# A decoder layer with routed experts: two kinds of DRAM writes move to another queue, and the embedding's four pieces move along the program

## The chip, the cores and the metric

The kernel runs on 1 core of one Trainium2 chip. Its engines are TensorE (PE, with its weight loads shown as PEld), VectorE (DVE), ScalarE (ACT), GpSimd (POOL) and SyncE (SP); each works through its own queue in order, and a DMA (a transfer between DRAM and SBUF) is issued from the queue of SP, ACT or POOL. The metric is device time in microseconds (us), less is better. The kernel before takes 1480.44 us, the median of 3 runs (1479.26 to 1485.14).

## The reference, cut to what matters

One layer over 512 tokens of width 2048, all float32:

```
y = concat(s5(u), conformer_conv(v, g)) @ w_o + b_o
h = layer_norm(ALPHA * x + y)                        # residual 1
# routing: softmax over 4 groups, top 1; 8 experts in it, top 2
t = h;  g_p, g_idx = top_1(softmax(t @ w_rg + b_rg))
e_val, e_idx = top_2(t @ w_re + b_re, within the group)
combine = softmax(e_val) * g_p
m = sum_e combine[e] * ((silu(t @ w_gate[e]) * (t @ w_up[e])) @ w_down[e])
h = layer_norm(ALPHA * h + m)                        # residual 2
e = (p @ w_p) * sigmoid(h @ w_pg + b_pg)             # p: (512, 256), the embedding
x = layer_norm(ALPHA * h + e)
```

There are 32 experts of hidden width 256, and each expert's three matrices are 6 MB, so the expert stage reads 192 MB of weights.

## The kernel before, in words

The tokens are NT = 4 tiles `tt[m]` of 128 rows. The kernel runs in stages: input projection and the two head groups, output projection with the first norm, routing, the expert stage, and the tail with the gate product and the last norms. This change is in the routing and at the start of the expert stage.

At the end of the output projection `finish` and `normalize` turn `tt[m]` into h; line 877 writes each tile to DRAM (`h_dram`, 1 MB each) from ACT's queue, since the experts fetch their tokens from there by an indirect gather. The routing is a chain of small DVE and PE steps: choices (`oh`, line 955), counts (lines 958 to 966 on PE), the rank of each chosen expert (`rtok`, line 991), one-hot rows (`slot_hot`), and two small products (lines 196 and 203) that give the slot tables `sl0` (whom to gather) and `wt0` (their weights).

The embedding's product p @ w_p depends on nothing of this. Its four row pieces m = 0 to 3 are placed where PE may be idle: `embedding(m, x)` (line 828 on) builds a zero `z` from column `x`, adds it to piece m of p on ACT (line 833), so that the product can't start before `x` exists, multiplies (line 839), copies the result out of PSUM on ACT (line 840) and writes it to `p_dram` in two writes of 512 KB (line 841, ACT's queue). Before, piece 0 is tied to a column of the logits `lg`, piece 1 to `cmax` (line 1033), piece 2 to `wt0`. Piece 3 stands behind the first expert group, lines 1172 to 1179; there the copies go into a tile `pe` that exists once, so the second pair of copies waits until the first write has been read out.

The expert stage has 13 groups (`GROUPS`); group 0 has two experts that are fixed beforehand, the others are read from a table that the routing makes. A group gathers its token rows (line 1069, POOL's queue, into `gx`), transposes them (`xtp`, line 1083), runs up and gate (`gu`, line 1103), the activation, and down (`dps`, line 1123), and scatters 2 x 512 KB to `y_dram` (line 1073, POOL's queue). Weights come in loads of 1 MB from SP's queue (line 1065) into a ring of 17 tiles: 15 named `ring`, and the 2 `raw` tiles, which hold w_p until the embedding's last product and join the ring behind it. The loads of group 0 (12) and the first three of group 1 are issued first.

Behind group 0 stands a branch, `tc.If(most > 0)` at line 1187, for tokens that don't fit; here it isn't taken. Every engine goes through it, and SP's way through waits until the transfers that ACT and SP have issued have landed. The tile framework places the instructions of each engine in an order of its own, and gives the DMAs of ACT and SP together eight completion counters in turn, so that at most eight of them are in flight and each one waits for the one eight places ahead; POOL's DMAs have eight others.

Lines that matter: 828 to 841, 877, 912 (piece 0), 1037 and 1038 (pieces 1 and 2), 1069, 1073, 1128 (clearing `gx`), 1148 to 1155, 1172 to 1181, 1187.

Of the kernel before, what the change touches and what calls it, by code (L numbers as in the profile page):

```python
# [8 lines left out]
FT = mybir.dt.float32  # L9
# [8 lines left out]
P = 128  # L18
# [8 lines left out]
NT = S // P  # L27
NE = 32
FH = 256
ALPHA = 2.0 ** 0.25  # L30
# [24 lines left out]
def build(tc, I, out, dbg=None, stages=9):  # L55
    nc = tc.nc
    V = nc.vector
    A = nc.scalar
    G = nc.gpsimd
    T = nc.tensor  # L60
# [147 lines left out]
    h_dram = dpool.tile([S, D], FT, name="h_dram")  # L208
    p_dram = dpool.tile([NT, 4, P, 512], FT, name="p_dram")
# [6 lines left out]
    wt0 = cpool.tile([P, NGR], FT, name="wt0")  # L216
# [27 lines left out]
    def bank(name, bufs=1):  # L244
        if name in bturn:

            n = bturn[name]
            bturn[name] += 1
            name, bufs = (("zp", 4) if n % 5 < 4 else ("xp", 1)) if name == "ops" else (("wps", "cps")[n % 2], 1)
        return psA.tile([P, 512], FT, name=name, tag=name, bufs=bufs)  # L250

    if True:
        with ExitStack() as s2:
# [151 lines left out]
            for j in range(3):  # L405
                m = 1 << j
# [191 lines left out]
            for s_, f in enumerate(order):  # L598
# [17 lines left out]
                ps = w_in_mm(w_first if s_ == 0 else next(w_in))  # L616
# [19 lines left out]
    tt = [tp_.tile([P, D], FT, name=f"tt{m}") for m in range(NT)]  # L636
    s1 = top.enter_context(ExitStack())
    if True:
# [36 lines left out]
        ps = bank("htp")  # L675
# [30 lines left out]
        rs_, ps = rows  # L706
# [3 lines left out]
        for q in range(4):  # L710
            hl = next(w_in)
            for f in range(2):
                wh, wl = hl[f]
                ps = bank("ops")
# [22 lines left out]
        with ExitStack() as s3:  # L737
# [24 lines left out]
            ps = bank("yp")  # L762
# [22 lines left out]
        with ExitStack() as s3:  # L785
# [5 lines left out]
            lg = op_.tile([P, NT, 36], FT, name="lg")  # L791
# [36 lines left out]
            def embedding(m, x):  # L828

                z = op_.tile([P, 1], FT, name="pz0", bufs=1)  # L830
                V.tensor_scalar(z, x, 0.0, 0.0, op0=OP.is_equal, op1=OP.mult)
                pm = wB.tile([P, 2, P], FT, name="pm", tag="whi", bufs=4)
                A.activation(pm, pT[:, :, m * P:(m + 1) * P], AF.Identity, bias=z)
                for q in range(2):
                    pe_ = wB.tile([P, 2, 512], FT, name="pe", tag="wlo", bufs=4)
                    for c in range(2):
                        ps = bank("ops")
                        for k in range(2):
                            T.matmul(ps, pm[:, k], wps[q][:, k, c * 512:(c + 1) * 512], start=k == 0, stop=k == 1)
                        A.copy(pe_[:, c], ps)  # L840
                    A.dma_start(p_dram[m, 2 * q:2 * q + 2].rearrange("c p d -> p c d"), pe_)

            def logits(m, c):

# [27 lines left out]
            def normalize(m, mean, rstd):  # L872
                for q in range(4):
                    i = slice(q * 512, (q + 1) * 512)
                    t = tt[m][:, i]
                    layer_norm(t, t, mean, rstd, g1[:, i], b1[:, i])
                A.dma_start(h_dram[m * P:(m + 1) * P], tt[m])
                dump("h", tt[m], lambda d: d[m * P:(m + 1) * P])

            for c in range(4):  # L880
# [5 lines left out]
                ps = [bank("ops") for _ in range(NT)]  # L886
# [20 lines left out]
            pT = wB.tile([P, 2, S], FT, name="pT", tag="whi", bufs=4)  # L907
            nc.sync.dma_start(pT, I["pT"])
            wps = []
            for q in range(2):  # L910
                wps.append(raw_load(I["w_p"][q]).rearrange("p (k n) -> p k n", k=2))
            embedding(0, lg[:, NT - 1, 0:1])


            rp = Carve(scr)
# [67 lines left out]
            over, rtok, wts = sv[:, 0], sv[:, 1], sv[:, 2].rearrange("p (j t) -> p j t", j=2)  # L983
# [5 lines left out]
            V.tensor_reduce(pos, pt2, axis=AX.X, op=OP.add)  # L989
            V.tensor_tensor(pt, oo, rr[:, 0:NE].unsqueeze(1).unsqueeze(1).broadcast_to(e2), op=OP.mult)  # L990
            V.tensor_reduce(rtok, pt2, axis=AX.X, op=OP.add)
            by_place, pw = rp1.tile([P, 2 * NT, NP], FT), rp.tile([P, 2 * NT, NP], FT)
            pb = [P, 2 * NT, NP]
            V.tensor_tensor(by_place, rank.unsqueeze(1).broadcast_to(pb), rtok.unsqueeze(2).broadcast_to(pb), op=OP.is_equal)
# [34 lines left out]
            gcn, cmax = rt("gcn", NP), rt("cmax", 1)  # L1029
# [4 lines left out]
            V.tensor_copy(tab[:, NP:2 * NP], gcn)  # L1034
            V.tensor_copy(tab[:, 2 * NP:], cmax)
            A.dma_start(sv_dram, sv.rearrange("p a n -> p (a n)"))
            embedding(1, cmax)
            embedding(2, wt0[:, 0:1])
            dump("sl0", sl0); dump("wts", wts)

    psA_.close()
# [5 lines left out]
    if True:  # L1047
        psE = s5.enter_context(tc.tile_pool(reuse_waits="tile", name="psE", bufs=1, space=PSUM))
        ep = s5.enter_context(tc.tile_pool(reuse_waits="tile", name="ep", bufs=1))
# [95 lines left out]
            return [ring_load(part(expert(i, j), q)) for j in range(len(GROUPS[i][1]))]  # L1145

        early = [loads(0, q) for q in range(6)]
        pm3 = ep.tile([P, 2, P], FT, name="pm3")
        nc.sync.dma_start(pm3, I["pT"][:, :, (NT - 1) * P:])
        for m in range(NT):  # L1150
            A.mul(tt[m], tt[m], ALPHA)
        gather(sl0[:, 0:1])
        V.tensor_copy(ids_, tab[:, 0:NP])
        columns()
        for i, (width, members) in enumerate(GROUPS):
# [13 lines left out]

            ahead1 = [loads(1, q) for q in range(3)]  # L1170

            for q in range(2):
                pe_ = ep.tile([P, 2, 512], FT, name="pe")
                for c in range(2):
                    ps = bank("dps", 4)
                    for k in range(2):
                        T.matmul(ps, pm3[:, k], wps[q][:, k, c * 512:(c + 1) * 512], start=k == 0, stop=k == 1)
                    (A.copy if c else V.tensor_copy)(pe_[:, c], ps)
                A.dma_start(p_dram[NT - 1, 2 * q:2 * q + 2].rearrange("c p d -> p c d"), pe_)
            ring.extend(rpool.tile([P, D], FT, name="raw", tag="raw", bufs=2) for _ in range(2))  # L1180
            ahead1 += [loads(1, q) for q in range(3, 5)]

# [63 lines left out]
    with ExitStack() as s5:  # L1246
# [28 lines left out]
        for n in range(8):  # L1275
            ps = bank("fps", 6)
# [187 lines left out]
```

## Time and profile before

| | |
|---|---|
| median of 3 runs | 1480.44 us |
| profiled execution: its time, its span | 1482.75 us, 1480.9 us |
| PE busy | 1262.3 us (85%) |
| DVE, ACT, POOL busy | 778.5, 372.5, 382.7 us |
| moved | 349.34 MB, 236 GB/s over the span |
| mean granted TensorE clock | 0.926 |

In 40 slices of 37 us of the span, the DMA engines and what they moved look so:

```
DMA  6344445445632351147799999999999986426413
GB/s 233 112 131 118 150 122 156 142 117 174 246 123 85 114 210 57 44 170 284 298 422 420 420 420 416 418 417 414 415 411 411 411 351 235 142 107 213 142 44 121
```

From slice 20 on, at about 740 us, they move 411 to 422 GB/s for twelve slices: this is the expert stage. The rows further down are of the stretch just ahead of it, 600 to 745 us, and of the stage itself. Times in them are us from the start of the span. A row of the timeline is: start, duration, engine, line and operation, what it writes and reads, how many in a row, and in brackets how long the engine stood idle before it and what ended that.

### The profile page before, as it was taken

What the parts mean: (1) busy time and instruction counts of PE and PEld (TensorE: products, weight loads), DVE (VectorE), ACT (ScalarE), POOL (GpSimd) and SP (SyncE); (2) the same over time, 40 slices, a digit from 0 to 9 for tenths busy, and PEclk for the clock granted to TensorE, in tenths of its full rate; (3) what the DMA queues carried; (4) which work ended last, traced back from release to release, by engine and by line L of the source; (5) the groups of instructions that cost most, each with busy time, mean ns of one, the idle gap of its engine ahead of it and who ended that gap; (6) DMA issues with size and microseconds to landing.
All of it is one profiled execution on the core that took longest, in us unless ns stands there. A gap on an engine that the chain in (4) does not pass through costs nothing. (4 is left out here: it accounts for less than half of the span.)

```text
span 1480.9 us, 16676 instructions
## 1 busy us (share of the span) xinstructions
PE 1262.3 (85%) x6206; PEld 805.9 (54%) x6207; DVE 778.5 (53%) x1251; ACT 372.5 (25%) x559; POOL 382.7 (26%) x313
## 2 busy tenths in 40 slices
PE   6999999998999999968598998777676775599996
PEld 4887877887777888844243332221111111388884
DVE  7999899879998653681111110000000006985467
ACT  4335565544433432031001110000000003023210
POOL 0367768673945300000001111000000005700000
PEclk9998999998999999978899999898899986699998
DMA  6344445445632351147799999999999986426413
GB/s 233 112 131 118 150 122 156 142 117 174 246 123 85 114 210 57 44 170 284 298 422 420 420 420 416 418 417 414 415 411 411 411 351 235 142 107 213 142 44 121
DMA packets 97769, 349.34 MB, mean 236 GB/s; under 512 B 29705, under 2 KB 43529, under 8 KB 62097
## 3 DMA queue, kind: packets, MB, share of 16 engines
q1 hardware_dynamic: 51152, 303.21, 52.7%
q10 hardware_dynamic: 40912, 28.20, 6.6%
q0 software_dynamic: 5616, 16.79, 2.9%
q8 instruction: 51, 0.84, 0.2%
q14 instruction: 38, 0.30, 0.1%
HBM read 323.30 MB, written 35.34 MB: 242 GB/s over the span
## 5 line engine op out<-in xcount | busy, mean ns | idle before, releaser
L1103 PE MATMUL gu<-ring,xt 128*32 128x512 f32 (+2 forms) x1144 | 237.9, 671 | 58.7 <-DMA ring<-w_gu 58.7
L236 DVE SCALAR_TENSOR_TENSOR cps<-hc,wdw,cps 128x512 f32<-128x512 f32 x232 | 174.5, 752 | 4.8
L1103 PEld LDWEIGHTS gu<-ring,xt 128*32 128x32 f32 (+2 forms) x1144 | 58.7, 127 | 200.2 <-issue 100.2
L100 PE MATMUL zp<-xh,whi 128*128 128x512 f32 x384 | 157.5, 411 | 11.3 <-ACT whi L79 10.2
L79 ACT CAST whi<-raw 128x1024 fp32r<-128x1024 f32 x116 | 119.5, 1049 | 169.7 <-PE zp L102 55.7
L102 PE MATMUL zp<-xh,wlo 128*128 128x512 f32 x384 | 155.2, 404 | 1.5 <-DVE wlo L80 1.5
L101 PE MATMUL zp<-xl,whi 128*128 128x512 f32 x384 | 154.9, 403 | 1.6 <-DVE xl L80 1.6
L80 DVE TENSOR_TENSOR wlo<-raw,whi 128x1024 fp32r<-128x1024 f32 x90 | 123.8, 1386 | 55.3 <-ACT whi L79 54.4
L1109 DVE TENSOR_TENSOR act<-act,gu 128x256 f32<-128x256 f32 x13 | 5.5, 421 | 268.9 <-ACT act L1108 268.9
L1123 PE MATMUL dps<-ring,at 128*32 128x512 f32 (+2 forms) x568 | 113.6, 612 | 12.1 <-DMA ring<-w_dn 7.0
L1073 POOL DMA_INDIRECT y_dram<-ob,sl x26 | 25.6, 985 | 367.6 <-ACT ob L1125 358.0
L80 POOL TENSOR_TENSOR wlo<-raw,whi 128x1024 fp32r<-128x1024 f32 x26 | 72.4, 2787 | 85.8 <-ACT whi L79 73.3
L100 PE MATMUL fps<-whi,h2h 128*128 128x512 f32 x224 | 89.2, 399 | 0.7 <-ACT h2h L79 0.7
L102 PE MATMUL fps<-whi,h2l 128*128 128x512 f32 x224 | 89.3, 399 | 0.0
L100 PEld LDWEIGHTS zp<-xh,whi 128*128 128x128 f32 x384 | 74.6, 194 | 26.0 <-ACT whi L79 10.3
L101 PE MATMUL fps<-wlo,h2h 128*128 128x512 f32 x224 | 88.7, 397 | 0.0
L102 PEld LDWEIGHTS zp<-xh,wlo 128*128 128x128 f32 x384 | 74.6, 194 | 18.2 <-DVE wlo L80 2.4
L101 PEld LDWEIGHTS zp<-xl,whi 128*128 128x128 f32 x384 | 74.6, 194 | 16.8 <-DVE xl L80 2.0
L1123 PEld LDWEIGHTS dps<-ring,at 128*32 128x32 f32 (+2 forms) x568 | 31.7, 120 | 81.8 <-issue 54.5
L1125 DVE COPY ob<-dps 128x512 f32<-128x512 f32 x26 | 18.0, 692 | 108.5 <-PE dps L1123 108.5
L1088 DVE COPY xt<-xtp 128x512 f32<-128x512 f32 x26 | 18.0, 692 | 107.5 <-PE xtp L1083 107.5
L1069 POOL DMA_INDIRECT gx<-h_dram,sl x13 | 13.7, 1052 | 195.9 <-PE xtp L1083 133.2
(449 smaller groups left out, 2306.2 us busy)
## 6 DMA issues: line engine op xcount, KB each, us to landing
ring<-w_gu SPq DMA_DIRECT2D x114, 1024.0 KB
ring<-w_dn SPq DMA_DIRECT2D x56, 1024.0 KB
raw<-w_in SPq DMA_DIRECT2D x24, 1024.0 KB
raw<-w_o SPq DMA_DIRECT2D x16, 1024.0 KB
raw<-w_gu SPq DMA_DIRECT2D x14, 1024.0 KB
raw<-w_pg SPq DMA_DIRECT2D x14, 1024.0 KB
raw<-w_dn SPq DMA_DIRECT2D x8, 1024.0 KB
raw<-y_dram SPq DMA_DIRECT2D x12, 512.0 KB
```

The source lines that it names most:

```text
L79: A.copy(hi, src)
L80: eng.tensor_tensor(lo, src, hi.bitcast(FT), op=OP.subtract)
L100: T.matmul(ps, lh, rh, start=start, stop=False)
L101: T.matmul(ps, lh, rl, start=False, stop=False)
L102: T.matmul(ps, ll, rh, start=False, stop=stop)
L236: V.scalar_tensor_tensor(ps if k < 30 else acc, hc[:, k:k + S], wdw[:, ct, k:k + 1], ps, op0=OP.mult, op1=OP.add)
L1069: G.indirect_dma_start(out=gx, out_offset=None, in_=h_dram, in_offset=bass.IndirectOffsetOnAxis(ap=ig, axis=0), bounds_check=S - 1, oob_is ...
L1073: G.indirect_dma_start(out=y_dram[q], out_offset=bass.IndirectOffsetOnAxis(ap=isc, axis=0), in_=ob[:, q * 1024:(q + 1) * 1024], in_offset= ...
L1088: V.tensor_copy(o, ps)
L1103: T.matmul(gu[cols], xt[:, k, cols], raws[j][:, kk * 512:(kk + 1) * 512], start=k == 0, stop=k == KD - 1)
L1123: T.matmul(outs[c][cols], at[:, k, cols], raws[j][:, o:o + 512], start=k == 0, stop=k == 1)
L1125: (A.copy if c else V.tensor_copy)(ob[:, q * 1024 + c * 512:q * 1024 + (c + 1) * 512], outs[c])
```

## The change

Four edits. The writes of line 841 and line 877 are issued from GpSimd's queue. `embedding(0)` is tied to a column of `rtok` and stands behind it; `embedding(1)` is tied to `wt0`; what was tied to `cmax` is gone. Pieces 2 and 3 are both multiplied behind group 0, from one load of 256 columns of p, and their four writes go through GpSimd's queue. The scaling of the residual, `tt[m] * ALPHA` on ACT, is written behind these pieces.

```diff
@@ embedding(m, x) and normalize(m, ...)
-                    A.dma_start(p_dram[m, 2 * q:2 * q + 2].rearrange("c p d -> p c d"), pe_)
+                    G.dma_start(p_dram[m, 2 * q:2 * q + 2].rearrange("c p d -> p c d"), pe_)
...
-                A.dma_start(h_dram[m * P:(m + 1) * P], tt[m])
+                G.dma_start(h_dram[m * P:(m + 1) * P], tt[m])
@@ the routing
-            embedding(0, lg[:, NT - 1, 0:1])
...
             V.tensor_reduce(rtok, pt2, axis=AX.X, op=OP.add)
+            embedding(0, rtok[:, 0:1])
...
             A.dma_start(sv_dram, sv.rearrange("p a n -> p (a n)"))
-            embedding(1, cmax)
-            embedding(2, wt0[:, 0:1])
+            embedding(1, wt0[:, 0:1])
@@ the expert stage
         early = [loads(0, q) for q in range(6)]
-        pm3 = ep.tile([P, 2, P], FT, name="pm3")
-        nc.sync.dma_start(pm3, I["pT"][:, :, (NT - 1) * P:])
-        for m in range(NT):
-            A.mul(tt[m], tt[m], ALPHA)
+        pm = ep.tile([P, 2, 2 * P], FT, name="pm")
+        nc.sync.dma_start(pm, I["pT"][:, :, 2 * P:])
         gather(sl0[:, 0:1])
...
-            for q in range(2):
-                pe_ = ep.tile([P, 2, 512], FT, name="pe")
-                for c in range(2):
-                    ps = bank("dps", 4)
-                    for k in range(2):
-                        T.matmul(ps, pm3[:, k], wps[q][:, k, c * 512:(c + 1) * 512], start=k == 0, stop=k == 1)
-                    (A.copy if c else V.tensor_copy)(pe_[:, c], ps)
-                A.dma_start(p_dram[NT - 1, 2 * q:2 * q + 2].rearrange("c p d -> p c d"), pe_)
+            for m in range(2):
+                for q in range(2):
+                    pe_ = ep.tile([P, 2, 512], FT, name="pe")
+                    for c in range(2):
+                        ps = bank("dps", 4)
+                        for k in range(2):
+                            T.matmul(ps, pm[:, k, m * P:(m + 1) * P], wps[q][:, k, c * 512:(c + 1) * 512], start=k == 0, stop=k == 1)
+                        (A.copy if c else V.tensor_copy)(pe_[:, c], ps)
+                    G.dma_start(p_dram[2 + m, 2 * q:2 * q + 2].rearrange("c p d -> p c d"), pe_)
+            for m in range(NT):
+                A.mul(tt[m], tt[m], ALPHA)
```

How this moves instructions is best seen in three places. First PE in the routing; `zp`, `xp` and `yp` are PSUM banks, line 839 is the embedding, and the rows of before run from piece 0 to the small product of line 1028:

```order
L839 MATMUL zp<-raw,pm 128x512 x4
L839 MATMUL xp<-raw,pm 128x512 x2
L839 MATMUL zp<-raw,pm 128x512 x2
L958 MATMUL zp<-ones,scr 32x1 x4
L960 MATMUL zp<-scr,ones 128x32 x4
L964 MATMUL yp<-scr,tri 128x128
L966 MATMUL yp<-scr,ones 128x96
L966 MATMUL yp<-scr,ones 128x64
L966 MATMUL yp<-scr,ones 128x32
L978 MATMUL zp<-scr,ones 128x32
L979 MATMUL xp<-ones,scr 32x1
L1028 MATMUL zp<-scr,ones 128x104
```

The same stretch of PE now (some line numbers are one less):

```order
L957 MATMUL zp<-ones,scr 32x1 x4
L959 MATMUL zp<-scr,ones 128x32 x4
L963 MATMUL yp<-scr,tri 128x128
L965 MATMUL yp<-scr,ones 128x96
L965 MATMUL yp<-scr,ones 128x64
L965 MATMUL yp<-scr,ones 128x32
L977 MATMUL xp<-scr,ones 128x32
L978 MATMUL zp<-ones,scr 32x1
L839 MATMUL zp<-raw,pm 128x512 x6
L839 MATMUL xp<-raw,pm 128x512 x2
L1028 MATMUL zp<-scr,ones 128x104
L196 MATMUL cps<-rsc_5367 128x26 x8
```

Piece 0 went from ahead of the counts to behind the ranks; the slot product of line 196 now follows it directly, where before piece 1 stood ahead of that product.

Second POOL, from the end of the norm's constants to the gather of group 0 (`gx` is the gathered rows, `sl_76` the slot table, `pe` the embedding's product):

```order
-L1128 MEMSET gx 128x2048
-L1069 DMA gx<-h_dram,sl_76 128x2048
-L1073 DMA y_dram_70<-ob,sl_76 1024x1024
-L1073 DMA y_dram_71<-ob,sl_76 1024x1024
+L877 DMA h_dram<-tt_3353 128x2048
+L877 DMA h_dram<-tt_3354 128x2048
+L877 DMA h_dram<-tt_3355 128x2048
+L877 DMA h_dram<-tt_3356 128x2048
+L841 DMA p_dram<-pe 128x2x512 x4
+L1127 MEMSET gx 128x2048
+L1068 DMA gx<-h_dram,sl_76 128x2048
```

Eight writes now stand ahead of the clearing of `gx` and of group 0's gather on this queue, among them the two of the piece that is tied to `wt0`.

Third ACT, from the transposed columns of group 0 to the branch (`ob` is the group's output, `dps` PSUM banks):

```order
-L1086 COPY xt<-xtp 128x512 x2
-L1108 ACTIVATE act<-gu 128x256
-L1114 COPY at<-atp 128x256
-L1125 COPY ob<-dps 128x512 x2
-L1178 COPY pe<-dps 128x512
-L1179 DMA p_dram<-pe 128x2x512
-L1178 COPY pe<-dps 128x512
+L1085 COPY xt<-xtp 128x512 x2
+L1107 ACTIVATE act<-gu 128x256
+L1113 COPY at<-atp 128x256
+L1124 COPY ob<-dps 128x512 x2
+L1176 COPY pe<-dps 128x512 x4
```

Where two copies with one write between them stood ahead of the branch, four copies stand now, with three writes between them on POOL. The scalings of the residual don't appear here: the framework still places them in the routing, each behind the write of its tile.

## Rows read from the trace of the kernel before

**Rows 1.** Busy time, clock (PEclk), DMA share and rate by stretch.
```profile
719.00:734.00 15.00, 6.65 (x16) 2.66 (x14) 1.38 (x2) 1.40 (x3) 2.00 (x2) 0.87 0.58 196
734.00:745.00 11.00, 5.04 (x13) 2.99 (x14) 0.69 (x1) 0.59 (x1) 0.00 (x0) 0.55 0.95 355
745.00:1230.00 485.00, 381.78 (x2025) 114.92 (x2024) 42.77 (x71) 36.04 (x70) 34.05 (x34) 0.93 0.99 409
```

**Rows 2.** Waits of SP's queue, 600 to 740 us: total, times, longest.
```profile
SPq L1065 <- DMA h_dram<-tt: 49.0, 1, 49.0
SPq L1065 <- DMA p_dram<-pe: 34.9, 6, 9.5
```

**Rows 3.** Timeline behind group 0, all engines.
```profile
718.52 7.13 PE L1177 MATMUL dps<-raw,pm 128*128 128x512 f32 x16
...
722.26 0.59 ACT L1178 COPY pe<-dps 128x512 f32<-128x512 f32 x1 [3.03 <-PE dps L1177]
...
722.87 0.37 ACTq L1179 DMA_DIRECT2D p_dram<-pe  x1
...
725.68 0.33 SPq L1065 DMA_DIRECT2D raw<-w_dn  x1
730.85 0.59 ACT L1178 COPY pe<-dps 128x512 f32<-128x512 f32 x1 [8.01 <-DMA p_dram<-pe]
730.90 0.69 DVE L1178 COPY pe<-dps 128x512 f32<-128x512 f32 x1 [9.66 <-DMA p_dram<-pe]
732.95 1.03 POOL L1069 DMA_INDIRECT gx<-h_dram,sl  x1 [12.48 <-DVEq L1187]
...
734.25 0.35 SPq L1065 DMA_DIRECT2D ring<-w_dn  x1
...
739.18 1.09 PE L1083 MATMUL xtp<-ident,gx 128*128 128x128 f32 x4 [13.53 <-DMA gx<-h_dram,sl]
...
741.96 4.56 PE L1103 MATMUL gu<-ring,xt 128*128 128x512 f32 x8
```

**Rows 4.** The branch's line: SP's steps through it, first and last start.
```profile
L1187 SPq EVENT_SEMAPHORE  x9: 17/17/17, 731.3 to 734.0; - x9
```

**Rows 5.** Timeline of DVE in the routing.
```profile
660.05 0.15 DVE L973 COPY scr<-zp 32x1 f32<-32x1 f32 x1 [3.75 <-PE zp L958]
...
663.63 0.40 DVE L991 TENSOR_REDUCE scr<-scr 128x8 f32<-128x256 f32 x1
...
669.26 1.23 DVE L190 TENSOR_TENSOR rsc<-iof,scr 128x1024 f32<-128x1024 f32 x1
...
681.09 0.17 DVE L204 COPY wt<-wps 128x13 f32<-128x13 f32 x1 [1.16 <-PE wps L203]
```

**Rows 6.** Timeline of PE from the routing into group 1.
```profile
668.72 7.14 PE L839 MATMUL zp<-raw,pm 128*128 128x512 f32 x12 [4.50 <-ACT pm L833]
...
677.41 1.86 PE L196 MATMUL cps<-rsc 128*128 128x26 f32 x16
...
682.12 8.83 PE L839 MATMUL zp<-raw,pm 128*128 128x512 f32 x16 [1.06 <-ACT pm L833]
691.62 0.66 PE L1083 MATMUL xtp<-ident,gx 128*128 128x128 f32 x4 [0.68 <-ACT pe L840]
...
746.80 3.60 PE L1103 MATMUL gu<-ring,xt 128*128 128x512 f32 x8
```

**Rows 7.** Timeline of POOL ahead of group 0.
```profile
628.81 1.81 POOL L1128 MEMSET gx<- 128x2048 f32 x1 [92.40 <-DVE lnf L159]
680.84 1.26 POOL L1069 DMA_INDIRECT gx<-h_dram,sl  x1 [50.21 <-DMA p_dram<-pe]
```

**Rows 8.** Issue to landing of POOL's transfers: scatter (line 1073), then gather (tile gx).
```profile
DMA to landing us min/median/max: 3.8/3.8/3.8
DMA to landing us min/median/max: 6.1/9.8/10.0
```

**Rows 9.** Waits of SP's queue for PE, 734 to 875 us: total, times, longest.
```profile
SPq L1065 <- PE gu L1103: 11.5, 7, 4.4
```

## The prediction

> **What bounds the kernel now.** I read the page's slices first: DMA engines full from about 740 us on. Then the busy times by stretch [rows 1]: from 745 to 1230 us the DMA share is 0.99 at 409 GB/s while PE is busy 382 of 485 us. The expert stage waits for its weights, so each us by which the loads resume later behind group 0 is a us at the end, unless more of them have landed by then. Ahead of it stands a hole: from 719 to 734 us the share is 0.58 [rows 1], although group 0's twelve ring tiles are free.
>
> The timeline shows what holds it [rows 3]. The embedding's last piece multiplies from 718.52 to 725.65; then the two raw tiles are free, and the last load that doesn't wait for the branch is issued at 725.68. The first copies into `pe` end at 722.85, their write is issued at 722.87, and the second copies wait for it until 730.85, 8.0 us. Then the branch: SP steps through it from 731.3 to 734.0 [rows 4], the gather of group 1 goes out at 732.95, and SP's next load at 734.25 [rows 3]. So the end hangs on two things: when the second raw load goes out (SP has to see it landed), and when the last copy into `pe` is done.
>
> SP's long waits lie earlier: 49.0 us for a write of h and 34.9 us for writes of the embedding [rows 2], because its loads take counters that these writes hold. They look like the profile's biggest loss, but the ring has 17 tiles, and all 17 are filled before the branch as it is; filled sooner they stay full.
>
> **The change part by part.** The sum is made in the profiled execution (1482.75 us, span 1480.9); the median of the runs shown is 2.3 us below it, and I put the difference on the median.
>
> *Writes off ACT's queue.* SP's 83.9 us of waits go. By the placement in the section on the change and the program's waits, the first loads need none of these writes any more, so seven of group 0's twelve loads can land before the routing. Worth nothing, since group 0 doesn't wait for them before (PE goes from its transposes into `gu` without a DMA wait), and the ring's size caps what is landed at the branch.
>
> *Routing.* Before, DVE stands 3.75 us for the counts, which wait on PE behind piece 0 [rows 5]. That goes; with shorter waits behind it I take 5 us (3.75 to 5.5). `rtok`, at 664.03 before, is there at 659.0. Piece 0 now starts on PE 0.9 us later (as from `wt0`, done at 681.26, to PE at 682.12 [rows 5, 6]), takes 8.7 us (668.72 to 677.41 [rows 6]) and ends at 668.6; with the small product of line 1028, 0.4 us, the slot product starts at 669.0, against 677.41. The one-hot rows it needs, done at 670.49 before [rows 5], come 5 us earlier too and don't bind. So `wt0` is there at 672.9, 8.4 us earlier (7.2 to 9.0).
>
> *Group 0's start.* This gain doesn't reach group 0. On POOL the gather now stands behind all four embedding writes and the clearing of `gx`, and the last two writes are of the piece that waits for `wt0`. Step by step: `wt0` 672.9, PE 673.7, its 8.83 us [rows 6] to 682.6, the last copy 0.59 [rows 3] to 683.2, the write's issue on POOL, for which I take an indirect one's 1.03 us [rows 3], to 684.3, the clearing 1.81 us [rows 7] to 686.1, and the gather's landing. Before, the gather went out at 680.84 [rows 7], beside piece 2 on PE. POOL's gathers take 6.1 to 9.8 us [rows 8]; half a ring of loads goes out in that moment but the stage isn't full yet, so 7. The transposes start at 693.2, against 691.62 [rows 6]: 1.6 us later, after 10 us in which PE is idle. Behind the 13.5 us hole at 739 the granted clock is 0.55 over the stretch [rows 1], close to the lower of its two levels (1.2 of 2.4 GHz), the first transposes take 1.09 us instead of 0.66, the first eight `gu` 4.56 instead of 3.60 [rows 3, 6]; that is 1.4 us more, which I add. Group 0 ends 3.0 us later. Bounds: -0.6 (routing at 9.0, a landing of 6.1, an issue as short as ACT's 0.37, though the cold clock stays) to +8.6 (routing at 7.2, a landing of 9.8, an issue of 2 us, 2 us of clock).
>
> The Trainium skill, "DMA: Bandwidth & Descriptors", section "Anatomy of one DMA - SWDGE (gpsimd) path", gives a DMA from GpSimd's queue about 2.0 us plus its bytes at 436 GB/s: an estimate of 4.4 us for the gather and 3.2 us for a write of 512 KB, where the rows have 6.1 and 3.8. By that rule group 0 would start 2.6 us sooner and the result would be 1488.4; the row is this kernel's, so I keep it.
>
> *Two pieces behind group 0.* The second piece adds 16 passes on PE, 7.13 us as the first [rows 3]. The raw tiles come free only behind them, so the last load ahead of the branch goes out 7.1 us later than group 0's end makes it: 10.1 us in all, at 735.8. Its last two products need PSUM banks that the second pair of copies empties, which wait for the first write; at 3.8 us a write, as POOL's scatter of equal size [rows 8], this is in time; at the 8.0 us of before it costs 2.4 us. From that load to SP's next one behind the branch it took 8.6 us (725.68 to 734.25 [rows 3]); I keep that, with bounds of -1.5 (a transfer of its size lands in 6.1 us [rows 8], and one us for the steps) and +2.4. SP resumes at about 744.4.
>
> *The copies' chain.* Four pairs of copies share one `pe`, so three writes stand between them ahead of the branch, one before. A link is 0.3 us to the issue, 3.8 us, and 0.7 us of copy: the first copies end at 725.9, the fourth pair starts at 739.6, and by the 2.05 us from copy to gather of before and 1.03 for the fourth write, now ahead of it on POOL, group 1's gather goes out at 742.7. Under resumed loads it lands in 9.8 us [rows 8]: 752.5, against 739.04, 13.4 us later, 3.3 us behind the loads. Up to eight loads are in flight, 20 us of transfer at 409 GB/s, and SP waits for PE's freeing of tiles 4.4 us at the longest [rows 9]; 3.3 us more mostly hide under what is in flight. I take 0.5 (0 to 5).
>
> *Residual scaling.* The placement leaves it in the routing, each behind its tile's write: nothing, and nobody on PE waits for it.
>
> **Sum:** 3.0 + 7.1 + 0 + 0.5 = 10.6 us. The profiled execution would take 1493.4; on the median, 1480.4 + 10.6 = **1491**. By the bounds: -0.6 + 7.1 - 1.5 = +5.0 at the least, 8.6 + 7.1 + 2.4 + 2.4 + 5 = +25 at the most.
>
> **The rivals.** About 0.5% (7.4 us) is what a measurement of this kernel tells from no change.
>
> *A, the forecast:* group 0 a little late, PE's second piece in full, 1488 to 1495. Chance 0.51.
>
> *B, the serial writes decide.* If a POOL write takes the 8.0 us that ACT's took beside a raw load [rows 3], three links are 12.6 us longer, the gather lags the loads by 16 us, and the load queue, some 10 us of which can be spared, runs dry: 6 to 10 us on top, 1497 to 1501. For it: two raw loads go out just then. Against: before, both fell on one write, now they are spread over three. Chance 0.17. The Trainium skill, "SBUF - State Buffer", section "SBUF: two separate sides", warns that some VectorE instructions keep GpSimd from writing a DMA's descriptors. In this stretch DVE is busy 1.38 of 15 us [rows 1], so it adds little to B.
>
> *C, the lower bounds together:* short landings, quick steps through the branch: +4 to +7.4 us, 1484.5 to 1487.8. Chance 0.22.
>
> *D, not slower: the routing's 8.4 us reach group 0.* It needs the gather out before the last embedding writes, landed when PE ends piece 1 at 682.6. Then the transposes start at 683.3, 8.3 us earlier, the second piece takes 7.1 back, and the result is about 1479. For it: the gather waits for `sl0` alone; against: POOL's order. It decides from the moment the gather's issue is ahead of 677. Chance 0.06.
>
> *E, faster: the loads count.* Seven or eight tiles landed early, 1.05 MB each at 409 GB/s, 2.6 us a tile, up to 20 us: 1460 to 1472. It would need the ring not to be full at the branch; all 17 loads are out at 725.68, and the hole of 719 to 734 speaks against it. Chance 0.04.
>
> **How the numbers follow.** Slower by over 0.5% is A but for its lowest edge, and B: 0.68. Within 0.5% is C, D and that edge: 0.28. Faster is E: 0.04. The predicted time is A's, 1491. The range 1483 to 1501 leaves out D, E and the top of B.
>
> **What would show it.** In the profile after: SP's loads `ring<-w_gu` issued from about 602 us on, none waiting for h or the embedding; DVE's long wait for line 958's counts gone; `wt0` near 673; POOL's gather near 686, behind the clearing; `xtp` near 693; sixteen more passes of the embedding behind group 0; four copy pairs with waits for a write between them; SP's first load behind the branch near 744 and PE's next transposes near 752; from there the same rate to the end and an unchanged tail. A gather before 680, or a branch passed before 738, makes the forecast wrong; PE waiting for tiles in groups 1 to 3 with DMA idle would be B.

## The result, and the profile after

The changed kernel takes 1499.18 us (median of 4 runs, 1498.29 to 1500.74), beside 1482.06 us (4 runs, 1479.26 to 1485.14) for the kernel before: a ratio of 1.0113, 95% interval 1.0093 to 1.0133. The kernel before has one run more here than ahead of the prediction, which moves its median from 1480.44 to 1482.06. The change makes it 17 us slower; the forecast was 1491, 10.6 us slower. The two profiled executions, 1498.47 and 1482.75 us with spans of 1496.6 and 1480.9 us, are 15.7 us apart, and that is what the readings below divide up. The changed kernel's timeline runs 1.15 us ahead as the routing begins (SP's load of `pT` is issued at 600.63, before at 601.78), which makes the later differences that much larger than the raw times show.

The timeline of the kernel after, all engines, from the routing to group 1 (columns: start, duration, engine, line, operation, tiles, count, and in brackets the engine's idle time before it and what ended it):

```profile
652.71 1.91 PE L959 MATMUL zp<-scr,ones 128*128 128x32 f32 x8
...
659.54 8.21 PE L839 MATMUL zp<-raw,pm 128*128 128x512 f32 x12 [2.46 <-ACT pm L833]
...
671.59 3.19 PE L203 MATMUL wps<-rsc 128*128 128x13 f32 x16
675.85 6.88 PE L839 MATMUL zp<-raw,pm 128*128 128x512 f32 x12 [1.07 <-ACT pm L833]
...
688.19 1.10 POOL L1068 DMA_INDIRECT gx<-h_dram,sl  x1 [0.29 <-POOL gx L1127]
694.18 1.09 PE L1082 MATMUL xtp<-ident,gx 128*128 128x128 f32 x4 [9.73 <-DMA gx<-h_dram,sl]
...
716.00 8.78 PE L1122 MATMUL dps<-ring,at 128*64 128x512 f32 x32 [0.46 <-ACT at L1113]
724.71 14.00 PE L1175 MATMUL dps<-raw,pm 128*128 128x512 f32 x32
735.31 0.35 SPq L1064 DMA_DIRECT2D raw<-w_gu  x1
738.74 0.33 SPq L1064 DMA_DIRECT2D raw<-w_dn  x1
739.48 0.71 POOL L1177 DMA_DIRECT2D p_dram<-pe  x1 [4.92 <-DVE pe L1176]
747.84 0.71 POOL L1177 DMA_DIRECT2D p_dram<-pe  x1 [7.65 <-ACTq L1187]
747.98 0.35 SPq L1064 DMA_DIRECT2D ring<-w_dn  x1
748.86 1.08 POOL L1068 DMA_INDIRECT gx<-h_dram,sl  x1 [0.31 <-issue]
762.35 1.09 PE L1082 MATMUL xtp<-ident,gx 128*128 128x128 f32 x4 [23.64 <-DMA gx<-h_dram,sl]
```

Read it from the bottom. SP's first load behind the branch goes out at 747.98, before at 734.25 [rows 3]: 13.73 us later. Going up: its last load ahead of the branch at 738.74 (before 725.68), when the embedding's 32 passes behind group 0 free the raw tiles; these passes start at 724.71 (before 718.52), 6.19 us later, and the added 16 make the rest; group 0's transposes start at 694.18 (before 691.62 [rows 6]), behind a gather that POOL issues at 688.19 instead of 680.84 [rows 7].

Busy times of the kernel after by stretch (length, then busy us and count of PE, its weight loads, DVE, ACT, POOL; PE's granted clock, DMA share, GB/s):

```profile
652.00:659.00 7.00, 4.89 (x28) 4.66 (x28) 5.14 (x32) 0.50 (x2) 0.00 (x0) 0.50 0.00 1
669.00:676.00 7.00, 5.93 (x37) 5.34 (x35) 1.89 (x12) 1.09 (x2) 0.73 (x1) 0.72 0.37 145
684.00:694.00 10.00, 0.45 (x2) 0.00 (x0) 0.00 (x0) 0.59 (x1) 3.64 (x3) 0.75 0.77 243
694.00:725.00 31.00, 28.05 (x115) 9.98 (x116) 3.82 (x7) 2.68 (x6) 1.04 (x1) 0.86 0.44 181
712.00:725.00 13.00, 11.08 (x43) 3.39 (x40) 2.29 (x4) 1.51 (x4) 1.04 (x1) 0.87 0.05 20
719.00:745.00 26.00, 19.71 (x58) 7.69 (x54) 3.46 (x5) 2.93 (x5) 4.29 (x5) 0.96 0.46 159
745.00:1246.00 501.00, 385.22 (x2040) 116.88 (x2040) 45.36 (x75) 37.16 (x72) 36.01 (x36) 0.91 0.98 404
```

The last row is the expert stage behind the branch, with DMA as full as before [rows 1]: its last product ends 498.1 us after SP's resume, before 497.3. So the 15.7 us are 13.7 of a later resume, 0.8 inside the stage, and 1.1 behind it.

### The profile page after: what moved, and what is told of

Its sections match the earlier page's. It is cut to its first block, busy times and chain, and to the rows that moved or that the text cites. A ratio compares the mean times of both kernels' runs of the same rounds, so it can differ in the third digit from the quotient of the medians.

```text
span 1496.6 us, 16685 instructions
## 1 busy us (share of the span) xinstructions
PE 1259.4 (84%) x6206; PEld 803.3 (54%) x6207; DVE 780.2 (52%) x1252; ACT 370.7 (25%) x556; POOL 394.0 (26%) x325
## 4 chain that ended last, share of the span: by engine, by line
DMA 25%; PE 20%; DVE 4%; issue 1%; ACT 0%; POOL 0%; DVEq 0%; SPq 0%; POOLq 0%; ACTq 0%
DMA ring<-w_gu 13%; DMA ring<-w_dn 7%; PE gu L1102 5%; PE fps L102 3%; PE fps L100 3%; PE fps L101 3%; DMA raw<-w_gu 3%; PE dps L1122 3%; DMA gx<-h_dram,sl 1%; PE xtp L1082 1%; DVE tt L181 1%; DVE tt L180 1%; DVE lny L170 1%; DMA p_dram<-pe 1%; PE h2p L101 0%
## 5 line engine op out<-in xcount | busy, mean ns | idle before, releaser
L1102 PE MATMUL gu<-ring,xt 128*32 128x512 f32 (+2 forms) x1144 | 233.4, 660 | 54.6 <-DMA ring<-w_gu 54.6
L100 PE MATMUL zp<-xh,whi 128*128 128x512 f32 x384 | 156.3, 408 | 10.6 <-ACT whi L79 10.5
L1122 PE MATMUL dps<-ring,at 128*32 128x512 f32 (+2 forms) x568 | 117.3, 635 | 12.7 <-DMA ring<-w_dn 7.6
L100 PEld LDWEIGHTS zp<-xh,whi 128*128 128x128 f32 x384 | 73.7, 192 | 25.4 <-ACT whi L79 10.6
L1082 PE MATMUL xtp<-ident,gx 128*128 128x128 f32 x208 | 35.5, 296 | 43.6 <-DMA gx<-h_dram,sl 33.4
```

Of the source, the lines that this page charges most:

```text
L100: T.matmul(ps, lh, rh, start=start, stop=False)
L1082: T.transpose(ps[:, kk * P:(kk + 1) * P], gx[:, k * P:(k + 1) * P], ident)
L1102: T.matmul(gu[cols], xt[:, k, cols], raws[j][:, kk * 512:(kk + 1) * 512], start=k == 0, stop=k == KD - 1)
L1122: T.matmul(outs[c][cols], at[:, k, cols], raws[j][:, o:o + 512], start=k == 0, stop=k == 1)
```

## The experiments

Two theories stood against each other. **Theory 1**, the prediction's: the end hangs on when SP's loads resume behind the branch. **Theory 2**, rival B: it hangs on the serial writes of the late pieces and on group 1's gather behind them. All edits below are to the changed kernel; times are medians, ratios those to the kernel before on the same chip. e1 to e4, e5 to e8 and e9 to e11 ran on three chips, where the kernel before took 1482.79, 1481.77 and 1483.34 us; the changed kernel has only its four runs from the result, so a difference to it of 2 or 3 us is weak, and the ratios are the better measure.

**e1: the writes of the piece behind `wt0` back on ACT's queue.**
```diff
-  G.dma_start(p_dram[m, 2 * q:2 * q + 2]..., pe_)
+  (A if m else G).dma_start(p_dram[m, 2 * q:2 * q + 2]..., pe_)
```


> Only the two writes of the piece tied to wt0 go back to ScalarE's queue; on GpSimd the gather of group 0 then stands behind two embedding writes instead of four. Theory 1 (group 0 starts when its gather lands, and the end moves with it): the gather's issue, 688.2 us in the changed kernel, comes near 680, xtp starts near 685.5 instead of 694.2, PE's clock isn't cold there, so group 0 ends 8 to 11 us earlier and the time is 1488 to 1491. Rival (group 0 is held by PE behind piece 1 or by its tiles, not by the gather): xtp is earlier by under 2 us, 1497 to 1499.

Measured: 1482.88 us, ratio 0.9999 (0.998 to 1.0018). The whole loss is gone, 5 us more than theory 1 gave. The timeline, POOL and PE:

```profile
674.22 1.10 POOL L1068 DMA_INDIRECT gx<-h_dram,sl  x1 [1.38 <-issue]
...
682.49 1.88 PE L839 MATMUL xp<-raw,pm 128*128 128x512 f32 x4
684.20 0.60 PE L1082 MATMUL xtp<-ident,gx 128*128 128x128 f32 x4
...
704.03 7.09 PE L1122 MATMUL dps<-ring,at 128*64 128x512 f32 x32 [0.46 <-ACT at L1113]
711.04 14.00 PE L1175 MATMUL dps<-raw,pm 128*128 128x512 f32 x32
...
733.98 0.35 SPq L1064 DMA_DIRECT2D ring<-w_dn  x1
```

The gather goes out at 674.22, 14 us earlier and not 8: the two writes of the first piece, still ahead of it on POOL, go out at 666.85 and 670.29, and the clearing of `gx` follows at once. It has landed when PE ends the piece, and the transposes follow without a wait. This is what rival D described (transposes at 683.3). Group 0 takes 26.8 us (684.20 to 711.04) instead of 30.5: 10.0 us of start and 3.7 us of length make 13.7 of the 14.0 us by which SP resumes earlier. The two late pieces are still there, and the kernel is level with the one before.

**e2: four targets for the four late pairs of copies** (two tiles `pe`, the halves of `gx`).
```diff
-  pe_ = ep.tile([P, 2, 512], FT, name="pe")
+  pe_ = gx[:, q * 1024:(q + 1) * 1024].rearrange(...) if m else ep.tile(..., name="pe", bufs=2)
```


> The four pairs of copies behind group 0 get four targets of their own (two tiles pe, the two halves of gx), so that none waits for a write. Theory 1 (what counts is when SyncE's loads resume, which hangs on PE's second piece and the second raw load): 0 to -2 us, 1497 to 1499, with SyncE's first load behind the branch still near 748. Theory 2 (the chain of serial writes and the late gather of group 1 decide, rival B of the prediction): the fourth copies are done near 739 instead of 747.3, group 1's gather goes out 8 us earlier, and the time falls by about 8 us, to 1491.

Measured: 1496.72 us (1491.46 to 1498.07), ratio 1.0086 (1.006 to 1.0112), 2.5 us below the changed kernel. No copy waits for a write, the last write goes out at 738.03 instead of 747.84, and yet group 1's gather leaves at 747.48: POOL's steps through the branch run from 739.1 to 745.9. SP resumes at 745.44, in a timeline that runs 1.14 us ahead of the changed kernel's. Theory 2's 8 us don't come. The chain may cost some 2 us, but the two ratios' intervals overlap, so that isn't settled.

**e3: one piece behind group 0.**
```diff
+  if m == 0: G.dma_start(p_dram[NT - 1]..., tt[m]...)      # in normalize
-  for m in range(2):                                       # the late pieces
+  for m in range(1):
```


> Leaves out the product of the embedding's last piece (its rows are filled early with a copy of h, by one more write on GpSimd in the routing's start): one piece behind group 0, as before the change, everything else as in the changed kernel. Theory 1 (PE's 7.1 us of the second piece delay the last raw load and with it the branch): the raw loads go out 7 us earlier, SyncE resumes near 741, 1491 to 1493. Theory 2 (serial writes): two links of the copies' chain go as well, about 12 us, 1486 to 1488. If neither counts: 1498 to 1500.

Measured: 1486.26 us, ratio 1.0017 (0.9999 to 1.0034). By its median this is theory 2's number, but the trace divides it otherwise: the second raw load goes out at 731.45, 7.29 us earlier, SP resumes at 739.56, 8.42 us earlier, the stage behind it is 2.1 us shorter and what follows the stage 2.2 us, which no theory touches and which lies within the spread of all runs (247.5 to 250.6 us). So the piece costs what PE takes for it; the rest, 1.1 us from the raw load to the resume and the 2.1 us in the stage, fits the two links fewer, but isn't told apart from them here.

**e4: the writes of `h` back on ACT's queue.**
```diff
-  G.dma_start(h_dram[m * P:(m + 1) * P], tt[m])
+  A.dma_start(h_dram[m * P:(m + 1) * P], tt[m])
```


> Only the writes of h go back to ScalarE's queue. Theory 1: SyncE again waits some 49 us for h's writes before its early loads, but the ring's 17 tiles are full at the branch all the same: 1499 plus or minus 1.5, the same as the changed kernel. Rival (the early loads, or the writes of h on GpSimd, are part of the difference): slower than the changed kernel by over 4 us if the early loads help, faster by over 4 us if GpSimd's writes of h cost.

Measured: 1497.98 us, ratio 1.009 (1.0063 to 1.0116), level with the changed kernel. SP's long wait is back, in four parts (waits of SP's queue, 600 to 700 us: total, times, longest):

```profile
SPq L1064 <- DMA h_dram<-tt: 45.2, 4, 22.3
```

45.2 us of waiting that cost nothing: moving `h` was worth nothing, as forecast. The test is mild, though: seven of the ring's loads are out by 653 us (in the changed kernel by 631), and counted from the load of `pT` the eighth goes out at the same time in both, 64.1 us behind it.

**e5: three pieces ahead.** One falls into PE's gap before the routing, one behind `rtok`, one behind `wt0` with its writes on ACT's queue, one stays behind group 0.
```diff
+  embedding(0, lg[:, NT - 2, 0:1])            # behind the loads of w_p
-  embedding(0, rtok[:, 0:1])
+  embedding(1, rtok[:, 0:1])
-  embedding(1, wt0[:, 0:1])
+  embedding(2, wt0[:, 0:1])                   # its writes: A.dma_start
-  for m in range(2):                          # the late pieces
+  for m in range(1):
```


> The changed kernel with three pieces of the embedding ahead of group 0 instead of two: one tied to lg of token tile 2, so that it falls into the gap that PE has before the routing (7.48 us in the changed kernel), one to rtok, one to wt0 with its two writes on ScalarE's queue as in e1; one piece stays behind group 0. Theory 1 (the end is where SyncE's loads resume, plus 746 us): the routing is 1 to 2 us later than in e1, group 0 ends near 712.5, the second raw load goes out near 719.5, SyncE resumes near 728, and the time is 1474 to 1478, below both kernels. Rival (the added piece delays the routing by its whole 8.7 us): the gain of one piece less behind group 0 is given back, 1481 to 1485.

Measured: 1473.56 us (1471.42 to 1475.83), ratio 0.9942 (0.9926 to 0.9959): faster than both kernels, 25.6 us below the changed one.

```profile
646.01 5.35 PE L839 MATMUL zp<-raw,pm 128*128 128x512 f32 x8
...
655.07 1.08 PE L960 MATMUL zp<-scr,ones 128*128 128x32 f32 x8
...
685.57 0.66 PE L1083 MATMUL xtp<-ident,gx 128*128 128x128 f32 x4 [0.68 <-ACT pe L840]
...
728.93 0.35 SPq L1065 DMA_DIRECT2D ring<-w_dn  x1
```

The piece in the gap delays the routing's first product there by little (654.73 instead of 652.19, in a timeline that starts 1.5 us later) and keeps PE's clock up for the counts: their eight passes of 128x32 take 1.08 us, as in no run where the gap is empty (1.91 in the changed kernel). The clock isn't kept beyond them: the next piece takes 10.20 us, in the changed kernel 9.9. Counted from the load of `pT`, group 0 starts 0.35 us earlier than in e1 and SP resumes 6.8 us earlier, which is what a piece behind group 0 takes on PE: the piece in the gap costs nothing, and the one less behind group 0 is gained in full.

**e6: all four pieces ahead,** two behind `wt0` with their writes on ACT's queue; the number that the branch tests has its own tile, written before group 0.
```diff
+  embedding(2, wt0[:, 0:1])
+  embedding(3, wt0[:, 0:1])                   # and none behind group 0
+  mo = ep.tile([P, 1], I32, name="mo")
```


> All four pieces ahead of group 0 (lg of tile 2, rtok, and two behind wt0 with their writes on ScalarE's queue), none behind it; the number that the branch tests gets a tile of its own, written before group 0. Theory 1: group 0 starts some 8.7 us later than in e5, near 694, but the raw loads wait for no product behind group 0, so SyncE passes the branch near 705 and refills the ring while group 0 runs. By resume plus 746 us that would be 1451; but group 1's gather comes only some 8 us earlier than before, and PE is busy 118 of 130 us in groups 1 to 3, so I expect 1455 to 1472. Rival (the branch still waits for the engines that work on group 0): SyncE resumes near 730, and the time is 1476 to 1485.

Measured: 1477.46 us (1473.72 to 1486.37), ratio 0.9977 (0.9958 to 0.9996). SP resumes at 729.08, so the rival's number came; but its last load ahead of the branch is out at 705.02. The last seven of the ring's loads had gone out only from 696.65 us on, behind waits for the writes of `sv_dram` and of the embedding, the DMA share is 1.00 or more from 700 to 720 us, and that last load took 21.1 us from issue to landing. So what SP waited for is its own loads; e10 tests it.

**e7 and e11: PE kept busy in the hole ahead of group 0,** by 20 and by 10 products that nothing reads.
```diff
+  keep = bank("dps", 4)                       # ahead of group 0's transposes
+  for _ in range(20):                         # e11: range(10)
+      T.matmul(keep, ident, wps[0][:, 0, 0:512], start=True, stop=True)
```


> The changed kernel with 20 products that nothing reads on PE between the last early piece and group 0's transposes, so that PE isn't idle while the gather lands. Theory 1 (the 3.6 us by which group 0 takes longer than in e1 are the clock's): xtp stays near 694, group 0 takes 26.9 us instead of 30.5, SyncE resumes near 744.5, 1495 to 1496. Rival (the ring's tiles or the late gather make group 0 longer): no change, 1498 to 1500.

> As e7 with 10 products instead of 20, since each took two passes there (17.3 us for the 20, and PE wasn't free when the gather landed): 8.7 us, which fits the hole. Theory 1 (the cold clock makes group 0 longer by 3.6 us): xtp as in the changed kernel, group 0 takes 26.9 us, SyncE resumes 3 to 4 us earlier, 1495 to 1496. Rival (the time isn't given back): 1498 to 1500.

Measured: e7 1499.4 us (ratio 1.0109, 1.0074 to 1.0145), e11 1495.48 us (ratio 1.0079, 1.0059 to 1.01). PE's rows, of e7 and then of e11:

```profile
686.13 17.33 PE L1152 MATMUL dps<-raw,ident 128*128 128x512 f32 x40
703.29 0.60 PE L1082 MATMUL xtp<-ident,gx 128*128 128x128 f32 x4
...
730.13 14.00 PE L1178 MATMUL dps<-raw,pm 128*128 128x512 f32 x32
```
```profile
683.95 8.75 PE L1152 MATMUL dps<-raw,ident 128*128 128x512 f32 x20
693.68 0.64 PE L1082 MATMUL xtp<-ident,gx 128*128 128x128 f32 x4 [0.99 <-DMA gx<-h_dram,sl]
695.17 0.66 PE L1082 MATMUL xtp<-ident,gx 128*128 128x128 f32 x4 [0.85 <-DVE xt L1087]
695.76 5.35 PE L1102 MATMUL gu<-ring,xt 128*64 128x512 f32 x16
...
722.26 14.00 PE L1178 MATMUL dps<-raw,pm 128*128 128x512 f32 x32
```

e7 had too many: each product is two passes, so PE was still busy over 7 us after the gather had landed, and no time came back; but group 0 took 26.8 us. With half of them the granted clock is 1.00 from 684 to 694 us, where the changed kernel has 0.75, and group 0 took 28.6 us instead of 30.5. One group of 16 passes took 5.35 us instead of 3.65: there, from 695.7 to 699.4, the granted clock is 0.61 and then 0.50 although PE is busy, and why it fell isn't shown. The median fell by 3.7 us, but the trace gives the products only the 2.0 us of group 0; the transposes also start 1.65 us earlier, counted from the load of `pT`, and that was gained ahead of the products (the slot product's passes of line 203 take 1.94 us instead of 3.19).

**e8: all writes of the embedding on ACT's queue.**
```diff
-  G.dma_start(p_dram[...]..., pe_)            # both places
+  A.dma_start(p_dram[...]..., pe_)
```


> All writes of the embedding, the two early and the two late pieces, back on ScalarE's queue; h stays on GpSimd's, the ties are those of the changed kernel. Theory 1 (only that the gather of group 0 isn't behind them matters): as e1, 1481 to 1485, SyncE's longer waits for the early writes cost nothing. Rival (writes on ScalarE's queue hold SyncE's loads back, and that counts): 1488 or more.

Measured: 1482.23 us, ratio 1.0 (0.9978 to 1.0021), as e1: moving the other writes as well gains nothing more. What counts is that the gather doesn't stand behind the late two.

**e9 and e10: e5 and e6 with SP's early loads freed.** The piece (e10: two) behind `wt0` is written into `ob` (and `pe`) in the expert stage's own code, so that its writes stand on POOL behind the gather; the write of `sv_dram` is on POOL too, and `pm` is loaded ahead of the ring.
```diff
+  for m in range(1):                          # behind gather(sl0); e10: range(2)
+      for q in range(2):
+          pe_ = ob[:, q * 1024:(q + 1) * 1024].rearrange(...)   # products, copies, write as behind group 0
-  A.dma_start(sv_dram, ...)
+  G.dma_start(sv_dram, ...)
```


> As e5, but the piece that stood behind wt0 with its writes on ScalarE's queue is now written into ob in the expert stage's own code, so that its writes stand behind the gather on GpSimd's queue, the write for sv_dram is on GpSimd's queue too, and the load of pm goes ahead of the ring's: none of SyncE's first loads needs a counter that such a write holds. Theory 1 with the rest that e5 and e6 left (SyncE resumes when all that it has issued has landed; in e5 twelve loads went out only from 692 us on, so DMA was still busy then): the ring is full when the last raw load goes out near 718, SyncE resumes 8 us later, near 726, and the time is 1469 to 1472. Rival (the early loads count for nothing, as in e4): 1472 to 1475 as e5.

> As e9, with the last piece too ahead of group 0 (into two tiles pe, writes behind the gather on GpSimd's queue) and none behind it; the number that the branch tests has its own tile, as in e6. If in e6 SyncE resumed at 729, 24 us after its last raw load, because the ring's loads went out late: it now resumes near 705 to 710, and group 1 is held by its gather, which goes out behind group 0's scatters near 720; PE starts group 1 near 728 instead of 733, 1462 to 1470. Rival (the branch itself waits for group 0's engines): SyncE resumes near 727, 1472 to 1477.

Measured: e9 1473.56 us (1468.46 to 1478.86), ratio 0.9925 (0.9898 to 0.9951), no gain over e5 that this resolves; its SP resumes at 730.39 and not near 726, so theory 1's number didn't come. e10 1472.49 us (1469.59 to 1473.14), 0.9924 (0.9902 to 0.9946). Its rows:

```profile
693.10 0.33 SPq L1064 DMA_DIRECT2D raw<-w_dn  x1
707.04 0.35 SPq L1064 DMA_DIRECT2D ring<-w_dn  x1
...
718.13 1.02 POOL L1072 DMA_INDIRECT y_dram<-ob,sl  x1 [2.39 <-ACT ob L1124]
729.54 1.05 POOL L1068 DMA_INDIRECT gx<-h_dram,sl  x1 [10.39 <-DMA y_dram<-ob,sl]
739.92 1.09 PE L1082 MATMUL xtp<-ident,gx 128*128 128x128 f32 x4 [22.74 <-DMA gx<-h_dram,sl]
```

SP now resumes at 707.04, as expected, while PE works on group 0 until 717, so the branch doesn't wait for group 0; e6 was late because its loads were. But the end didn't follow: POOL waits 10.39 us for group 0's scatter to land among the resumed loads before it issues group 1's gather, PE starts group 1 at 739.92, no earlier than before the change, and from 745 to 760 us the DMA share is 0.62. Here, for once, theory 2's gather is the bound.

**Both bounds in one table.** From the timelines: SP's resume R, PE's first transposes of group 1 X, the end of the stage's last product E.

| kernel | R | X | E | E - R | E - X |
|---|---|---|---|---|---|
| before | 734.25 | 739.18 | 1231.55 | 497.3 | 492.4 |
| after | 747.98 | 762.35 | 1246.11 | 498.1 | 483.8 |
| e1 | 733.98 | 749.78 | 1231.78 | 497.8 | 482.0 |
| e2 | 745.44 | 757.85 | 1240.79 | 495.4 | 482.9 |
| e3 | 739.56 | 747.41 | 1235.57 | 496.0 | 488.2 |
| e4 | 749.57 | 760.79 | 1246.77 | 497.2 | 486.0 |
| e5 | 728.93 | 733.30 | 1224.05 | 495.1 | 490.8 |
| e9 | 730.39 | 740.09 | 1226.61 | 496.2 | 486.5 |
| e10 | 707.04 | 739.92 | 1220.61 | 513.6 | 480.7 |

But for e10 the stage ends 495.1 to 498.1 us after SP's resume, wherever that lies, and it never ends under 480.7 us after PE's start on group 1 (the four kernels left out lie within the same bounds). The later of the two sums, R + 496 and X + 481, gives the end to about 2 us; only e10 shows the second by itself, so its constant rests on one kernel. In the changed kernel the two are level to 1 us (747.98 + 496 = 1244.0, 762.35 + 481 = 1243.4, where E is 1246.1). That fits e2, which has X 4.5 us and R 2.5 us lower (1.1 us of each by its earlier timeline), and whose median is 2.5 us less.

## Why the prediction was right, and where its sizes were off

The forecast's range, 1483 to 1501, holds 1499.18 with 2 us to spare; its number, 1491, is 8 us low. In the two traces, which it was worked out for, the slowdown is 15.7 us and not 10.6. Of these 5.1 us, group 0's later end is 3.2, the step to SP's resume 0.7, the stage 0.3 and what follows the stage 1.1, less 0.2 for the second piece. The other 3 us are the medians: the forecast put its own 2.3 us below the profiled time, as it was before the change, and the median after lies 0.7 us above it.

*The place of the loss* was right: a later group 0, the second piece in full, an end that follows SP's resume, and no gain from SP's 83.9 us of waits. e1, e3 and the table show the first three; e4 shows that the waits for h cost nothing. The sign that no load would wait for h or the embedding held for h alone. Seven loads were out by 631 us; the later ones found other waits, among them (waits of SP's queue in the kernel after, 600 to 740 us: total, times, longest):

```profile
SPq L1064 <- DMA sv_dram<-scr: 33.7, 1, 33.7
SPq L1064 <- DMA p_dram<-pe: 6.9, 1, 6.9
```

The last loads of group 0 and the first of group 1 were still out by 697 us, and from 712 to 725 the DMA share is 0.05: all of them had landed, and filled sooner the ring only stood full, as forecast.

*Second piece:* 7.1 us forecast, 6.9 measured (13.06 us between the last loads ahead of the branch, less the 6.19 of group 0), 7.3 in e3, whose timeline runs 0.5 us ahead. *From there to the resume:* forecast unchanged, 9.24 instead of 8.57 us.

*Group 0's start* was the mis-sized term: +3.0 forecast, +6.2 measured, inside the bounds of -0.6 to +8.6 (the lower one was added up wrong: with the 1.4 us of cold clock that it says stays, it is +0.8). Two steps of it failed by their size, both for the clock. First, `wt0` was to come 8.4 us earlier, and its copy on DVE is at 674.82, 6.3 us earlier. `rtok` was there when forecast (its last reduction ends at 658.8), but the piece that moved behind it had filled PE's gap before the routing. That gap is now 7.48 us of idle PE, the granted clock is 0.50 from 652 to 659 us, the lower of the two levels, and the first twelve passes of the piece take 8.21 us, before 7.14 [rows 6]. Then the slot product's last 16 passes take 3.19 us instead of 1.94, at a granted clock that was 1.00 from 669 to 671.5 us and 0.57 from 671.5 to 675. That the empty gap brings this second fall isn't shown: in e2, e8 and e11, with the same order, the passes take 1.94 us, and in e5, e9 and e10, with the gap filled, 2.41 to 2.55. Second, the clock was to cost 1.4 us in group 0; it cost 3.6 (30.5 us from the first transposes to the embedding, before 26.9; 26.8 in e1, e7 and e8, which have no hole ahead of it). 1.9 of them come right behind the hole, up to the end of the first 16 passes of `gu`. The other 1.7 are in the down products at 716.00, 8.78 us instead of 7.09, where the granted clock is 0.60 and 0.55 from 716 to 720 us although PE is busy. These needn't be the hole's: e9 has none and shows the same there,

```profile
706.30 8.79 PE L1122 MATMUL dps<-ring,at 128*64 128x512 f32 x32 [0.46 <-ACT at L1113]
```

and e2, with a hole of 10.79 us, doesn't (7.09). The landing was shorter than forecast, 6.0 us from issue to transposes, not 7. The Trainium skill, "DMA: Bandwidth & Descriptors", section "Anatomy of one DMA - SWDGE (gpsimd) path", by which I had estimated 4.4 us for the gather and 3.2 for a write of 512 KB, fits the shortest write here (3.1 us) and not the gather (5.9 us at the shortest).

*The copies' chain* came out later than forecast, and hid better. The writes on POOL took 3.1 to 9.4 us to land, the gather 13.4 (issue to landing, tile `pe` and tile `gx`, 600 to 800 us):

```profile
DMA to landing us min/median/max: 3.1/5.0/9.4
DMA to landing us min/median/max: 5.9/10.2/13.4
```

So group 1 starts 14.4 us behind the resume instead of 4.9, where 8 were forecast. The price stayed small, 0.8 us in the trace and perhaps 2 by e2, against 0.5 forecast with bounds of 0 to 5. SP's waits from 745 to 890 us show the lag, where before had 11.5 us [rows 9]:

```profile
SPq L1064 <- PE gu L1102: 61.2, 21, 4.9
```

The loads in flight covered it, down to the last 3 us that E - X leaves.

*The rivals.* B's mechanism is there, at part of its size: the three writes ahead of the branch took 3.1, 4.3 and 7.0 us to land and not 8.0 each, and group 1's gather lags the loads by 9.4 us more than before, not 16. Its price of 6 to 10 us didn't come, which agrees with the 10 us or so that it says can be spared. That the time lies in its 1497 to 1501 is chance, since the excess over the forecast is mostly group 0's and the medians'. D's forecast for group 0, transposes at 683.3, came within 1 us in e1 (684.20), where POOL's order is what it needed. E's early loads count only once nothing else holds the branch, and then e10 shows the next bound. The residual scaling stayed where it was, and cost nothing.

## What to carry to other kernels

An in-order queue that issues an urgent gather must not carry writes that wait for later work: here two writes ahead of it were worth 16 us, and where they went instead made no difference that was resolved (ACT's queue in e1, e5 and e8, behind the gather on POOL's in e9). Work that fills a gap of an engine can be free, and taking it out has a price of its own where the clock falls in the empty gap: behind 7.48 us of it, the counts' passes took 1.91 us instead of 1.08. Look at the granted clock of a gap before you move its filling elsewhere. Of two chains that end together, only the sum to the end tells which one to shorten: find in several runs the two constants behind them, and take the later.

## What the runs showed of the hardware

- A PE that was idle for 7.48 us had a granted clock of 0.50 in the 7 us behind, and the same passes took 1.91 us instead of 1.08; behind an idle 9.73 us, with a granted clock of 0.50 from 694.1 to 697.2, the transposes and products up to the end of the first 16 passes of `gu` took 7.6 us instead of 5.7.
- The granted clock also fell while PE was busy: 1.00 from 702.3 to 714 us, then 0.60 and 0.55 from 716 to 720, where 32 passes took 8.78 us instead of 7.09. PE had been idle for 1.46 and 0.46 us just ahead of them, as it is in e1, where they took 7.09. What brings the fall isn't shown.
- The same 512 KB write from POOL landed in 3.1 us on a quiet DMA and in 9.4 among resumed loads; the scatter of equal size in 3.2 and in 10.3 us (e10).
- A product of two float32 operands of 128x128 by 128x512 was two passes in the trace, some 0.44 us each at the full clock (32 in 14.00 us).
